# Stick-breaking attention with rounded-and-rest operands for the scores and a balancing rule for the copies

## The chip, the cores and the metric

One core of one Trainium2 chip runs the whole block as one program. The metric is the device time of the program in microseconds; lower is better. The kernel before was run three times: 3305.34, 3305.65 and 3313.6 us, median 3305.65.

## The reference

One layer of a hybrid encoder over 2048 tokens of width 1024, float32: a root-mean-square norm, one input projection, two groups of eight heads (a delta-rule recurrence and stick-breaking attention), one output projection, and a squared-ReLU MLP of width 4096. The change touches only the stick-breaking attention. For a block of 128 queries and all keys up to its end it is

```
z = einsum('bhqd,bhkd->bhqk', q, k) * scale          # head dimension 64
causal = key < query
log_beta = log_sigmoid(z)
log_keep = where(causal, log_beta - z, 0)
log_a = log_beta + reverse_cumsum(log_keep) - log_keep
att = where(causal, exp(log_a), 0)
out = einsum('bhqk,bhkd->bhqd', att, v)
```

So a weight is the sigmoid of a score times the product, over the keys between it and the query, of one minus their sigmoids.

## The kernel before, in words

The program has three stages on one core: stage 1 (norm, input projection, recurrence), stage 2 (the attention, `stage2`), stage 3 (output projection, MLP). Stage 1 writes queries, keys and values to DRAM, two heads to a tile of 128 partitions (64 rows each).

Stage 2 cuts the work into 40 pieces: a pair of heads `hp` (four of them), a block `b` of 512 queries, a block `j` of 512 keys with j from b down to 0. The piece with j equal to b is the diagonal one; 16 pieces are diagonal, 24 are not. A piece is four items, one for each 128 queries, so there are 160 items, counted by `k`. For a diagonal piece item i looks at W = 128(i+1) keys; everywhere else W is 512 ("full"). Of the 160 items, 112 are full.

For each item (lines are those of the kernel before; every instruction of the stage is issued through the helper `call` in `Ordered`, so the profile gives L259 for all of them, and they are told apart by their tiles):

- `scores` (L285): for each of the two heads one float32 matmul of the 64 rows of Q and K into the PSUM tile `z`, two buffers. A float32 matmul is two matmul instructions in the profile.
- `gates` (L293): ScalarE (ACT) computes `keep`, the sigmoid of minus the score, and `ga`, the sigmoid of the score, both from `z` and for both heads at once; on a diagonal item GpSimd (POOL) masks both; VectorE (DVE) runs for each head a reversed running product `E` over `keep`. The scan takes a column of `z` as its second operand.
- `product` (L311): POOL multiplies `ga` by the shifted `E`, one item later.
- Six items later (`lag=6`) the weights are turned: `turn` (L316) lets TensorE (PE) transpose blocks of `ga` into the PSUM tile `tr` (two buffers), and copies it to `th` in SBUF. An item has at most two such parts of 256 queries: the first part's copy runs on ACT, the second's on DVE.
- `values` (L329): PE multiplies `th` with V into the PSUM tile `OT`. `finish` (L338) turns and stores a finished block.

The order is written out by hand: `Ordered` chains all instructions of an engine in program order, so PE, ACT, DVE and POOL each run stage 2 as a fixed queue. One round k of the main loop issues, in this order: transposes and copy of the first part of item k-6; `values` of the second part that was turned in round k-1; the scores of item k; transposes and copy of the second part; the gates and scans of item k; the product of item k-1; and last `values` of the first part. So on PE the order in a round is: transposes of the first part, values of the last round's second part, z(k), transposes of the second part, values of the first part. The main loop's core:

```
first=turn(two[0],A) if two else None
if pend: done=values(*pend) or done
pend=None
z=scores(k) if k<n else None
if len(two)>1: pend=turn(two[1],V_)
if z is not None:
    new=gates(k,z)
    if prod: product(*prod)
    prod=new
...
if first: done=values(*first)
```

K, Q and V come by DMAs on SyncE's queue, issued in `load` by the scores of a piece's first item. Stage 3's first tiles are prepared on DVE, ACT and POOL in between, and its output projection follows when the attention is done.

Of the kernel before, what the change touches and what calls it, by code (L numbers as in the profile page):

```python
# [8 lines left out]
F32 = mybir.dt.float32  # L9
F32R = mybir.dt.float32r  # L10
BF16 = mybir.dt.bfloat16
AF = mybir.ActivationFunctionType
ALU = mybir.AluOpType
# [228 lines left out]
def stage2(tc,consts,kd,qd,vd,sbd,lag=6):  # L242

    nc=tc.nc
    with ExitStack() as ctx:
        sp=ctx.enter_context(tc.tile_pool(name="s2",bufs=1,reuse_waits="tile"))
        pz=ctx.enter_context(tc.tile_pool(name="p2z",bufs=1,reuse_waits="tile",space=PS))
        pp=ctx.enter_context(tc.tile_pool(name="p2",bufs=1,reuse_waits="tile",space=PS))  # L250
        pt=ctx.enter_context(tc.tile_pool(name="p2t",bufs=1,reuse_waits="tile",space=PS,side="right"))
        last={}
        class Ordered:

            def __init__(self,e): self.e=e
            def __getattr__(self,name):
                f=getattr(self.e,name)
                def call(*a,**k):
                    i=f(*a,**k)  # L259
                    if id(self.e) in last:  # L260
                        tc.add_manual_dep(i.ins,last[id(self.e)],mybir.DependencyInfo(mybir.DependencyClass.NoSync,mybir.DependencyReason.DATA),reason="program order")
                    last[id(self.e)]=i.ins.name
                    return i
                return call
        V_,A,P,TE=(Ordered(e) for e in (nc.vector,nc.scalar,nc.gpsimd,nc.tensor))

        keeps=[sp.tile([128,2,513],F32,name=f"keep{i}") for i in range(2)]
        for k in keeps: nc.gpsimd.memset(k[:,:,512:513],1.0)
        class Piece: pass
        pieces=[]  # L270

        for b,hp in [(b,hp) for two in ((0,2),(1,3)) for hp in range(4) for b in two]:
            for j in range(b,-1,-1):
                p=Piece(); p.b,p.hp,p.j,p.n=b,hp,j,f"{b}{hp}{j}"; p.gas=[]; pieces.append(p)
        def load(m):
            p=pieces[m]
            if p.j==p.b:
                p.Q=sp.tile([128,512],F32,tag="Q",name=f"Q{p.b}{p.hp}",bufs=2); p.carry=[None]*4; p.OT=[]
                nc.sync.dma_start(out=p.Q,in_=qd[p.hp][:,512*p.b:512*p.b+512])
            else: p.Q,p.carry,p.OT=pieces[m-1].Q,pieces[m-1].carry,pieces[m-1].OT  # L280
            p.K=sp.tile([128,512],F32,tag="K",name="K"+p.n,bufs=3); p.V=sp.tile([128,4,128],F32,tag="V",name="V"+p.n,bufs=5)
            nc.sync.dma_start(out=p.K,in_=kd[p.hp][:,512*p.j:512*p.j+512])
            nc.sync.dma_start(out=p.V,in_=vd[p.hp][:,4*p.j:4*p.j+4])
        def scores(k):
            p=pieces[k//4]; i=k%4  # L285
            if i==0: load(k//4)
            W=128*(i+1) if p.j==p.b else 512
            z=pz.tile([128,2,512],F32,tag="z",name=f"z{p.n}{i}",bufs=2)
            for h in range(2):
                TE.matmul(z[:,h,0:W],lhsT=p.Q[64*h:64*h+64,128*i:128*i+128],rhs=p.K[64*h:64*h+64,0:W],start=True,stop=True)  # L290
            return z
        def gates(k,z):
            p=pieces[k//4]; i=k%4; diag=p.j==p.b  # L293
            W=128*(i+1) if diag else 512; o=512-W
            s=keeps[k%2]
            A.activation(s[:,:,o:512],z[:,:,0:W],AF.Sigmoid,scale=-0.125)
            ga=sp.tile([128,2,512],F32,tag="ga",name=f"ga{p.n}{i}",bufs=11)
            A.activation(ga[:,:,o:512],z[:,:,0:W],AF.Sigmoid,scale=0.125)
            if diag:

                for t,fill in ((s,1.0),(ga,0.0)):
                    P.affine_select(t[:,:,384:512],t[:,:,384:512],pattern=[[0,2],[-1,128]],base=0,channel_multiplier=1,compare_op=ALU.is_gt,fill=fill)
            E=sp.tile([128,2,513],F32,tag="E",name=f"E{p.n}{i}",bufs=6)

            for h in range(2):
                init=1.0 if diag else p.carry[i][h]
                V_.tensor_tensor_scan(E[:,h,o:513][:,::-1],s[:,h,o:513][:,::-1],z[:,h,0:1].to_broadcast([128,W+1]),init,ALU.mult,ALU.bypass)
            p.carry[i]=[E[:,h,o:o+1] for h in range(2)]
            p.gas.append((ga,o))
            return ga,E,o  # L310
        def product(ga,E,o): P.tensor_tensor(out=ga[:,:,o:512],in0=ga[:,:,o:512],in1=E[:,:,o+1:513],op=ALU.mult)  # L311
        def parts(m):

            p=pieces[m//4]; kt=m%4; i0=kt if p.j==p.b else 0
            return [(p,kt,u,max(i0,2*u)) for u in range(2) if max(i0,2*u)<2*u+2]
        def turn(part,eng):  # L316
            p,kt,u,c0=part

            tr=pt.tile([128,2,256],F32,tag="tr",name=f"tr{p.n}{kt}{u}",bufs=2)
            for h in range(2):  # L320
                for i in range(c0,2*u+2):
                    ga,o=p.gas[i]
                    TE.transpose(tr[:,h,128*(i-2*u):128*(i-2*u)+128],ga[:,h,o+128*kt:o+128*kt+128],consts['ident'])
            th=sp.tile([128,2,256],F32,tag="th",name=f"th{p.n}{kt}{u}",bufs=4)
            q=slice(128*(c0-2*u),256)
            if eng is A: A.copy(th[:,:,q],tr[:,:,q])
            else: V_.tensor_copy(out=th[:,:,q],in_=tr[:,:,q])
            return part,th,q
        def values(part,th,q):  # L329
            p,kt,u,c0=part  # L330
            if p.j==p.b and kt==0 and u==0: p.OT.append(pp.tile([128,512],F32,tag="OT",name=f"OT{p.b}{p.hp}",bufs=2))
            for h in range(2):
                TE.matmul(p.OT[0][64*h:64*h+64,128*c0:256*u+256],lhsT=p.V[:,kt,64*h:64*h+64],rhs=th[:,h,q],start=p.j==p.b and kt==0 and u==0,stop=p.j==0 and kt==3 and u==1,skip_group_check=True)
            if p.j==0 and kt==3 and u==1:
                ots=sp.tile([128,512],F32,tag="ots",name=f"ots{p.b}{p.hp}",bufs=2)
                V_.tensor_copy(out=ots,in_=p.OT[0])
                return p,ots
        def finish(p,ots):  # L338
            o=pt.tile([128,4,128],F32,tag="tr",name=f"o{p.b}{p.hp}",bufs=2)
            for i in range(4): TE.transpose(o[:,i],ots[:,128*i:128*i+128],consts['ident'])  # L340
            osb=sp.tile([128,4,128],F32,tag="osb",name=f"osb{p.b}{p.hp}",bufs=2)
            A.copy(osb,o)
            nc.scalar.dma_start(out=sbd[512*p.b:512*p.b+512,128*p.hp:128*p.hp+128].rearrange("(i p) d -> p i d",i=4),in_=osb)
        n=4*len(pieces); pend=prod=done=out=None
        for k in range(n+lag+2):
            m=k-lag
            two=parts(m) if 0<=m<n else []
            first=turn(two[0],A) if two else None
            if pend: done=values(*pend) or done
            pend=None  # L350
            z=scores(k) if k<n else None
            if len(two)>1: pend=turn(two[1],V_)
            if z is not None:
                new=gates(k,z)
                if prod: product(*prod)
                prod=new
            elif prod: product(*prod); prod=None

            if out: finish(*out)
            out,done=done,None  # L360
            if first: done=values(*first)

# [388 lines left out]
```

## Time and profile before

| What | Value |
|---|---|
| Median of three runs | 3305.65 us |
| Own time of the profiled execution | 3306.65 us |
| Its span, first to last instruction | 3304.9 us |
| Mean granted TensorE clock | 0.976 |
| First scores of stage 2 / last scan of stage 2 starts | 1065.6 us / 1649.0 us |

The profile counts time from the span's start. "Busy" of an engine counts its own instructions, not its waits. A wait is put down to what ended last before the instruction started; that is inferred, and a name can be wrong where the engine named had long been done. Engines: PE is the matmul side of TensorE, PEld its weight loads, DVE VectorE, ACT ScalarE, POOL GpSimd.

### The profile page before, as it was taken

The page shows a single profiled execution, that of the slowest core. Times are in us where ns is not written, and L with a number is a line of the kernel's source. Part 1 is how long each engine was busy: PE and PEld are TensorE (multiplying, and loading weights), DVE is VectorE, ACT ScalarE, POOL GpSimd, SP SyncE. Part 2 cuts the span into 40 slices and gives each one's busy share as a digit, 9 for nine tenths or more (in the row PEclk, how much of TensorE's full clock was granted, in tenths as well). Part 3 has the DMA queues.
Part 4 walks back from the last instruction along what each step waited for, and adds up shares of the span by engine and source line. Part 5 has one row for each costly group of instructions (what it writes and reads, how often), then busy time and mean ns, then how long its engine had stood idle before and what let it go on. Part 6 is the DMA issues. An engine that isn't in the chain of part 4 may idle for free. (4 is left out here: it accounts for less than half of the span.)

```text
span 3304.9 us, 45571 instructions
## 1 busy us (share of the span) xinstructions
PE 3147.4 (95%) x17376; PEld 2373.0 (72%) x17376; DVE 2037.7 (62%) x3157; ACT 1147.4 (35%) x2172; POOL 1293.6 (39%) x1215
## 2 busy tenths in 40 slices
PE   8999999999999798899989999999999999999998
PEld 6677767777777443344467788888888888888887
DVE  4674575476376477888866555555555755555555
ACT  4434443443443366666632221111111411111112
POOL 5444443444443366766646322222221422222213
PEclk9989999999999799999999999999999999999999
DMA  3342242242234212111054121111111511111111
GB/s 100 103 118 75 86 128 77 77 127 86 69 97 119 63 61 68 58 52 58 27 175 161 64 77 51 51 52 52 45 45 45 171 66 51 51 51 46 41 43 64
DMA packets 153643, 251.90 MB, mean 76 GB/s; under 512 B 50768, under 2 KB 58960, under 8 KB 153424
## 3 DMA queue, kind: packets, MB, share of 16 engines
q1 hardware_dynamic: 144976, 244.78, 23.6%
q10 hardware_dynamic: 8448, 4.20, 0.5%
q8 instruction: 137, 2.24, 0.3%
q14 instruction: 82, 0.67, 0.1%
HBM read 202.72 MB, written 46.20 MB: 75 GB/s over the span
## 5 line engine op out<-in xcount | busy, mean ns | idle before, releaser
L158 DVE TENSOR_TENSOR acc<-acc,dn 128x512 f32<-128x512 f32 x512 | 344.5, 685 | 411.3 <-PE dn L32 404.8
L259 POOL TENSOR_TENSOR ga<-ga,E 128x1024 f32<-128x1024 f32 (+3 forms) x160 | 278.4, 1740 | 133.1 <-DVE E L259 76.5
L143 ACT ACTIVATE r<-up 128x512 f32<-128x512 f32 x128 | 75.7, 592 | 615.2 <-PE up L32 615.2
L146 DVE TENSOR_TENSOR m<-r 128x512 f32<-128x512 f32 x128 | 195.2, 1526 | 112.6 <-ACT r L143 112.6
L259 DVE TENSOR_TENSOR_SCAN E<-keep,E,z 128x513 f32<-128x513 f32 x192 | 234.5, 1267 | 45.8 <-ACT ga L259 25.6
L259 PE MATMUL OT<-th,V 128*64 128x256 f32 (+1 forms) x1152 | 183.7, 398 | 39.8 <-DVE th L259 31.2
L259 PEld LDWEIGHTS tr<-ident,ga 128*128 128x128 f32 x1088 | 114.8, 142 | 139.9 <-issue 123.4
L259 ACT ACTIVATE keep<-z 128x1024 f32<-128x1024 f32 (+3 forms) x160 | 144.0, 900 | 155.6 <-PE z L259 75.8
L259 PE MATMUL tr<-ident,ga 128*128 128x128 f32 x1088 | 183.9, 290 | 0.6 <-DVE th L259 0.6
L259 PE MATMUL z<-K,Q 64*128 64x512 f32 (+3 forms) x640 | 163.3, 587 | 19.3 <-DVE E L259 18.6
L147 DVE TENSOR_TENSOR gl<-m,gh 128x512 fp32r<-128x512 f32 x128 | 145.5, 1137 | 10.8
L259 ACT ACTIVATE ga<-z 128x1024 f32<-128x1024 f32 (+3 forms) x160 | 142.9, 893 | 0.0
L259 PEld LDWEIGHTS OT<-th,V 128*64 128x64 f32 x1152 | 57.6, 136 | 109.6 <-DVE th L259 49.9
L405 POOL TENSOR_TENSOR wls<-wfs,whs 128x512 fp32r<-128x512 f32 x64 | 84.7, 1324 | 101.8 <-ACT whs L404 94.7
L555 DVE TENSOR_TENSOR Xs<-Xs,tm 128x240 f32<-128x240 f32 (+27 forms) x248 | 118.5, 478 | 6.3
L554 DVE TENSOR_TENSOR tm<-Am,Xs 128x240 f32<-128x240 f32 (+27 forms) x248 | 103.2, 416 | 23.0 <-DMA Am<-scrA 16.7
L259 DVE TENSOR_TENSOR_SCAN E<-keep,z 128x129 f32<-128x129 f32 (+3 forms) x128 | 98.0, 807 | 26.9 <-ACT ga L259 14.9
L259 DVE COPY th<-tr 128x512 f32<-128x512 f32 x128 | 86.7, 677 | 41.5 <-PE tr L259 41.2
L30 PE MATMUL ips<-hT,whs 128*128 128x512 f32 x256 | 109.0, 426 | 0.0
L32 PE MATMUL ips<-hT,wls 128*128 128x512 f32 x256 | 108.9, 425 | 0.0
L30 PE MATMUL op<-wo,yh 128*128 128x512 f32 x256 | 103.8, 406 | 4.3 <-ACT wo L203 2.3
L31 PE MATMUL op<-wol,yh 128*128 128x512 f32 x256 | 104.1, 407 | 2.4 <-DVE wol L204 2.4
(1261 smaller groups left out, 8651.7 us busy)
## 6 DMA issues: line engine op xcount, KB each, us to landing
wfs<-w_in SPq DMA_DIRECT2D x64, 256.0 KB, 2.8
K<-kd SPq DMA_DIRECT2D x40, 256.0 KB, 2.8
V<-vd SPq DMA_DIRECT2D x40, 256.0 KB, 3.0
x<-x SPq DMA_DIRECT2D x32, 256.0 KB, 3.0
wfr<-w_in SPq DMA_DIRECT2D x32, 256.0 KB, 2.7
wfk<-w_in SPq DMA_DIRECT2D x32, 256.0 KB, 2.7
wfv<-w_in SPq DMA_DIRECT2D x32, 256.0 KB, 2.7
wfsv<-w_in SPq DMA_DIRECT2D x32, 256.0 KB, 2.9
```

What stands on the lines that cost most here:

```text
L30: nc.tensor.matmul(ps,lhsT=lh,rhs=rh,start=first,stop=False)
L31: nc.tensor.matmul(ps,lhsT=lh,rhs=rl,start=False,stop=False)
L32: nc.tensor.matmul(ps,lhsT=ll,rhs=rh,start=False,stop=last)
L143: A.activation(r,ps,AF.Relu)
L146: V.tensor_tensor(out=m,in0=r,in1=r,op=ALU.mult)
L147: V.tensor_tensor(out=gl[:,bl],in0=m,in1=gh[:,bl].bitcast(F32),op=ALU.subtract)
L158: V.tensor_tensor(out=a,in0=a,in1=ps,op=ALU.add)
L259: i=f(*a,**k)
L405: nc.gpsimd.tensor_tensor(out=wl,in0=wf,in1=wh.bitcast(F32),op=ALU.subtract)
L554: V.tensor_tensor(out=tm[:,0:m,i+1:],in0=Am[:,i,i+1:].unsqueeze(1).to_broadcast(sh),in1=X[:,0:m,i:i+1].to_broadcast(sh),op=ALU.mult)
L555: V.tensor_tensor(out=X[:,0:m,i+1:],in0=X[:,0:m,i+1:],in1=tm[:,0:m,i+1:],op=ALU.add)
```

## The change

Four things are done in `stage2`.

1. Scores. Q and K are fetched to `Qf` and `Kf` and split: ACT copies each to a rounded tile (`hi`, type float32r), POOL subtracts it from the original to give the rest (`lo`). A score is then three float32r matmuls accumulated in `z`: hi by hi, hi by lo, lo by hi, with the two heads' matmuls in turn.
2. Fetching. The DMAs of a piece are issued two pieces ahead (in round 2 of a piece), the split one piece ahead (in round 1 of a piece), at the end of the round.
3. Order. `keep` is issued right after the scores, ahead of the second part's transposes and copy; `ga` stays behind them.
4. Copies. Both copies of a round choose their engine by a running count of work: each `keep` adds an item's ACT and DVE work, each split adds 0.58 to ACT, and a copy goes to the engine whose count with the copy added is smaller.

```diff
+        load={"ACT":0.0,"DVE":0.0}
...
-        def load(m):
+        def fetch(m):
             p=pieces[m]
             if p.j==p.b:
-                p.Q=sp.tile([128,512],F32,tag="Q",name=f"Q{p.b}{p.hp}",bufs=2); p.carry=[None]*4; p.OT=[]
-                nc.sync.dma_start(out=p.Q,in_=qd[p.hp][:,512*p.b:512*p.b+512])
-            else: p.Q,p.carry,p.OT=pieces[m-1].Q,pieces[m-1].carry,pieces[m-1].OT
-            p.K=sp.tile([128,512],F32,tag="K",name="K"+p.n,bufs=3); p.V=sp.tile([128,4,128],F32,tag="V",name="V"+p.n,bufs=5)
-            nc.sync.dma_start(out=p.K,in_=kd[p.hp][:,512*p.j:512*p.j+512])
+                p.Qf=sp.tile([128,512],F32,tag="Q",name=f"Q{p.b}{p.hp}",bufs=1); p.carry=[None]*4; p.OT=[]
+                nc.sync.dma_start(out=p.Qf,in_=qd[p.hp][:,512*p.b:512*p.b+512])
+            else: p.Qf,p.carry,p.OT=None,pieces[m-1].carry,pieces[m-1].OT
+            p.Kf=sp.tile([128,512],F32,tag="K",name="K"+p.n,bufs=2); p.V=sp.tile([128,4,128],F32,tag="V",name="V"+p.n,bufs=5)
+            nc.sync.dma_start(out=p.Kf,in_=kd[p.hp][:,512*p.j:512*p.j+512])
             nc.sync.dma_start(out=p.V,in_=vd[p.hp][:,4*p.j:4*p.j+4])
+        def split(m):
+
+            p=pieces[m]
+            two=[("K",p.Kf)]+([("Q",p.Qf)] if p.Qf is not None else [])
+            for t,f in two:
+                hi,lo=(sp.tile([128,512],F32R,tag=t+x,name=t+x+p.n,bufs=2) for x in "hl")
+                A.copy(hi,f); load["ACT"]+=0.58
+                P.tensor_tensor(out=lo,in0=f,in1=hi.bitcast(F32),op=ALU.subtract)
+                setattr(p,t,(hi,lo))
+            if p.Qf is None: p.Q=pieces[m-1].Q
         def scores(k):
             p=pieces[k//4]; i=k%4
-            if i==0: load(k//4)
             W=128*(i+1) if p.j==p.b else 512
             z=pz.tile([128,2,512],F32,tag="z",name=f"z{p.n}{i}",bufs=2)
+            mms=[]
             for h in range(2):
-                TE.matmul(z[:,h,0:W],lhsT=p.Q[64*h:64*h+64,128*i:128*i+128],rhs=p.K[64*h:64*h+64,0:W],start=True,stop=True)
+                r=slice(64*h,64*h+64); q=slice(128*i,128*i+128)
+                mms.append([(p.Q[x][r,q],p.K[y][r,0:W],z[:,h,0:W]) for x,y in ((0,0),(0,1),(1,0))])
+            for c,both in enumerate(zip(*mms)):
+                for l,r,o in both: TE.matmul(o,lhsT=l,rhs=r,start=c==0,stop=c==2,skip_group_check=True)
             return z
+        def keep(k,z):
...
+            A.activation(s[:,:,o:512],z[:,:,0:W],AF.Sigmoid,scale=-0.125)
+            load["ACT"]+=2*(0.1+0.0018*W); load["DVE"]+=2*(0.05+0.0024*W)
         def gates(k,z):
...
-            A.activation(s[:,:,o:512],z[:,:,0:W],AF.Sigmoid,scale=-0.125)
...
-        def turn(part,eng):
+        def turn(part):
...
-            if eng is A: A.copy(th[:,:,q],tr[:,:,q])
-            else: V_.tensor_copy(out=th[:,:,q],in_=tr[:,:,q])
+            w=256*(2-(c0-2*u))
+            if load["ACT"]+0.15+0.0009*w<=load["DVE"]+0.12+0.0011*w: A.copy(th[:,:,q],tr[:,:,q]); load["ACT"]+=0.15+0.0009*w
+            else: V_.tensor_copy(out=th[:,:,q],in_=tr[:,:,q]); load["DVE"]+=0.12+0.0011*w
...
+        fetch(0); split(0); fetch(1)
         n=4*len(pieces); pend=prod=done=out=None
         for k in range(n+lag+2):
             m=k-lag
             two=parts(m) if 0<=m<n else []
-            first=turn(two[0],A) if two else None
+            first=turn(two[0]) if two else None
             if pend: done=values(*pend) or done
             pend=None
             z=scores(k) if k<n else None
-            if len(two)>1: pend=turn(two[1],V_)
+            if z is not None: keep(k,z)
+            if len(two)>1: pend=turn(two[1])
             if z is not None:
                 new=gates(k,z)
...
             if out: finish(*out)
+            if k%4==1 and k//4+1<len(pieces): split(k//4+1)
+            if k%4==2 and k//4+2<len(pieces): fetch(k//4+2)
```

## Rows read from the trace of the kernel before

**Rows 1.** The page: its head and the busy times of PE and DVE.

```profile
span 3304.9 us, 45571 instructions
...
PE 3147.4 (95%) x17376; PEld 2373.0 (72%) x17376; DVE 2037.7 (62%) x3157; ACT 1147.4 (35%) x2172; POOL 1293.6 (39%) x1215
```

**Rows 2.** Busy time by stretch: stage 2, a stretch of stage 3.

```profile
core 0: us, PE busy (x) PEld busy (x) DVE busy (x) ACT busy (x) POOL busy (x), PEclk, DMA share, GB/s
1140.00:1650.00 510.00, 463.81 (x2772) 214.22 (x2772) 410.78 (x452) 334.31 (x476) 322.78 (x275) 0.99 0.18 54
...
2000.00:2400.00 400.00, 400.00 (x1767) 331.34 (x1766) 226.43 (x240) 63.52 (x93) 91.55 (x37) 1.00 0.15 51
```

**Rows 3.** Timeline (start, duration): the round of item 124, item 125 begins.

```profile
1527.68 2.34 DVE L259 TENSOR_TENSOR_SCAN E<-keep,z 128x513 f32<-128x513 f32 x2 [0.82 <-ACT ga L259]
...
1527.82 1.13 PE L259 MATMUL z<-K,Q 64*128 64x512 f32 x4
...
1528.88 0.66 PE L259 MATMUL tr<-ident,ga 128*128 128x128 f32 x4
1529.04 1.03 ACT L259 ACTIVATE keep<-z 128x1024 f32<-128x1024 f32 x1 [0.98 <-POOL ga L259]
...
1529.46 0.65 PE L259 MATMUL OT<-th,V 128*64 128x256 f32 x4
1529.94 0.67 DVE L259 COPY th<-tr 128x512 f32<-128x512 f32 x1
1529.96 1.02 ACT L259 ACTIVATE ga<-z 128x1024 f32<-128x1024 f32 x1
...
1530.05 0.66 PE L259 MATMUL tr<-ident,ga 128*128 128x128 f32 x4
...
1530.66 0.65 PE L259 MATMUL OT<-th,V 128*64 128x256 f32 x4
1530.87 0.59 ACT L259 COPY th<-tr 128x512 f32<-128x512 f32 x1
1531.02 2.46 DVE L259 TENSOR_TENSOR_SCAN E<-keep,E,z 128x513 f32<-128x513 f32 x2 [0.41 <-ACT ga L259]
...
1531.24 1.13 PE L259 MATMUL z<-K,Q 64*128 64x512 f32 x4
...
1533.39 0.66 DVE L259 COPY th<-tr 128x512 f32<-128x512 f32 x1
...
1534.44 2.46 DVE L259 TENSOR_TENSOR_SCAN E<-keep,E,z 128x513 f32<-128x513 f32 x2 [0.39 <-ACT ga L259]
...
1534.69 1.13 PE L259 MATMUL z<-K,Q 64*128 64x512 f32 x4
```

**Rows 4.** Waits, 1140 to 1640 us: who waited for whom, total, times, longest.

```profile
DVE E L259 <- ACT ga L259: 37.4, 60, 1.3
...
PE OT L259 <- DVE th L259: 24.8, 27, 3.2
```

**Rows 5.** Timeline of PE: the score matmuls of item 125, head pairs apart.

```profile
1531.24 0.70 PE L259 MATMUL z<-K,Q 64*128 64x512 f32 x2
...
1531.77 0.60 PE L259 MATMUL z<-K,Q 64*128 64x512 f32 x2
```

**Rows 6.** Groups of instructions by line and shape (busy us, mean ns).

```profile
L405 POOL TENSOR_TENSOR wls<-wfs,whs 128x512 fp32r<-128x512 f32 x64 | 84.7, 1324 | 101.8 <-ACT whs L404 94.7 <-issue 4.0 <-ACT sg L470 2.6
...
L404 ACT CAST whs<-wfs 128x512 fp32r<-128x512 f32 x64 | 39.4, 616 | 70.1 <-issue 20.7 <-PE ips L31 18.8 <-PE ipsv L31 12.4
```

**Rows 7.** Busy time in two stretches of stage 2 (columns of rows 2).

```profile
1127.00:1134.00 7.00, 1.84 (x9) 0.69 (x9) 5.54 (x8) 1.07 (x2) 4.38 (x5) 0.50 0.42 135
...
1345.00:1352.00 7.00, 3.84 (x16) 1.35 (x14) 6.40 (x6) 1.37 (x3) 4.36 (x3) 0.76 0.38 114
```

**Rows 8.** Timeline: where stage 1's last chain ends and stage 2 takes over.

```profile
1113.17 1.91 PE L601 MATMUL Xp<-UV,P 128*64 128x64 f32 x16
...
1115.01 1.12 PE L259 MATMUL tr<-ident,ga 128*128 128x128 f32 x4
```

More of the change, by code (lines that the diff above doesn't have):

```diff
@@ L292, in gates @@
+            return z
+        def keep(k,z):
+            p=pieces[k//4]; i=k%4; diag=p.j==p.b
+            W=128*(i+1) if diag else 512; o=512-W
+            s=keeps[k%2]
+            A.activation(s[:,:,o:512],z[:,:,0:W],AF.Sigmoid,scale=-0.125)
+            load["ACT"]+=2*(0.1+0.0018*W); load["DVE"]+=2*(0.05+0.0024*W)
         def gates(k,z):
```

## The prediction

> **What bounds the kernel now.** I read the head of the page first: TensorE is busy 95% of the span, DVE 62% [rows 1]. A busy PE is not yet the bound, so the stages were read apart. In stage 2, the only one touched, PE is busy 463.8 of 510 us and no other engine over 411 [rows 2]. Then the timeline of one full off-diagonal round, that of item 124 [rows 3]. The reader should see that PE never pauses in it: scores at 1527.82, transposes 1.06 later, values 0.58 after, transposes 0.59, values 0.61, next scores 0.58: 3.42 us a round. But a loop through the other engines is just as long. A scan starts at 1531.02; 2.37 later DVE starts the second part's copy; 0.72 after a copy's start PE starts its values (1529.94 to 1530.66); 0.58 later come the scores; 1.22 after these `keep`, 0.92 later `ga`, 1.06 later the scan. That is 6.87 for two rounds, against 6.84 on PE. Both limits stand together, and a change has to shorten both.
>
> One thing in these rows decides the rest: the scan starts 0.04 after the end of `ga`, not after `keep`, though it reads only `keep`. Over the stage the scans are put down 60 times to `ga` as what ended last [rows 4], and none of the 160 items has a scan that starts ahead of its `ga`'s end. Both read the same PSUM tile `z`, and `ga` stands ahead of the scans in program order, as it does after the change.
>
> Items 0 to 5 run in the shadow of stage 1's last chain, up to 1115 [rows 8]; stage 3 waits for the last attention output. So what a round of stage 2 gains or loses from item 6 on reaches the end.
>
> **Scores.** Removed per full item: two float32 matmuls, each two passes. The first pair of passes (both heads at once) starts at 1531.24, the second at 1531.77 [rows 5]: 0.10 to load weights and 0.43 a pass, so 0.10 + 0.86, and 0.10 more until the transposes: 1.06. Added: three passes in float32r. No float32r matmul on 64 rows is in the trace; the nearest are stage 3's on 128 rows, 400 us for 1767, 0.226 each [rows 2]. If the heads still run together, that is 0.10 + 0.68 + 0.10 = 0.88, a gain of 0.18. The other end is heads in turn, 0.68 more. I take the first, as the float32 pair runs together [rows 5].
>
> Here the Trainium skill speaks against the change. In rows 5 the second pass follows 0.53 after the first, so its weight load lay under the first pass on the same rows of the array. "TensorE: Matmul & The Clock Gate" (Part 3, The mechanism) says that weight loads overlap matmuls in flight "only when row_grp differs". By that rule each later pass of a head would show its load, and the sum below would be +72 instead of +55; the trace disagrees for two passes, and no row shows three.
>
> A round on PE becomes 3.42 - 0.18 = 3.24. For 112 full items that is 20 us; the 32 with 256 or 384 keys give some 0.1 each, 3 us; the 16 with 128 keys I put at nothing, as there weight loads are as long as the passes. Values waited 24.8 us on PE for copies of DVE [rows 4], at the second part. That goes where ACT makes the copy; I take 16, since part of it lies in crowded stretches. Together 39 us less.
>
> **Second copies on ACT.** The rule, worked through with its own constants over the 160 items, gives ACT 101 of the 128 second copies. Such a copy stands between `keep` and `ga`. It holds ACT 0.50 (0.59, less the 0.1 by which ACT's instructions overlap, as 1.03 against 0.92 for `keep`) [rows 3], so `ga` and the scan come 0.50 later. By itself this costs nothing: from scores to scan is then 1.04 + 0.92 + 0.50 + 1.06 = 3.52, and with the scan's 2.46 that is 5.98 for the two `z` buffers, under 6.48. Its own loop (1.04 + 0.92 + copy 0.59 + 0.05 + values 0.58 = 3.18 a round) is just under 3.24.
>
> **First copies on DVE.** The same rule gives DVE 80 of the 160 first copies; all were ACT's. This is the term that decides. On DVE the first copy of round k stands behind the scans of item k-1. On PE its values stand ahead of the next round's transposes, the second part's values and the next scores: PE is in order, so all of these wait. The loop is now: scan to copy 2.37, copy to values 0.72, to transposes 0.59, to values 0.61, to scores 0.58, to `keep` 1.04, to second copy 0.92, to `ga` 0.50, to the scan of item k+1 1.06. That is 8.39 for two rounds, where PE needs 6.48: a price of 1.91 us [rows 3].
>
> It is paid once in two rounds, since a round that follows a held one starts late enough for its own copy. It is full where the scan ahead is 512 wide; behind scans of 128 or 256 it is next to nothing. Of the 80, 49 follow a full scan and no paying round. Five of these lie in the two stretches where stage 3's preparation and its DMAs already hold the stage (PE 1.84 and 3.84 of 7 us [rows 7]); I count nothing for them. 44 x 1.91 = 84 us more. Bounds: 44 x 0.5 if the scan no longer waited for `ga` (a rival below), and 60 x 1.91 = 115.
>
> **Splits.** 40 K and 16 Q tiles: 56 casts on ACT of 0.616 and 56 subtractions on POOL of 1.324 [rows 6], 34 and 74 us of work. ACT is busy 334 and POOL 323 of 510 [rows 2], so they lie beside other work. What can show: the cast is queued behind `ga` and ahead of the next first copy and `keep`. ACT is free 3.38 after a round's scores (1.04 + 0.92 + 0.50 + 0.92); with a first copy and one cast 4.40, with two 4.92, and `keep` is due at 4.28: at most 0.12 in 24 rounds and 0.64 in 15, 12 us. I take 5, as half of these rounds have the first copy on DVE. On POOL the masks of a diagonal item queue behind a subtraction: between 0 and 16 x 1.32 = 21 us; I take 5, because the product ahead of it usually ends early there. The DMAs (same number, same sizes) go out one to two pieces earlier on SP's queue, so K and Q cannot be later than now; nothing. Moving `keep` ahead of the second copy is what lets ACT take it, and costs nothing else.
>
> **Sum.** -39 + 84 + 10 = +55 on the profiled execution's own 3306.65, which is 1.0 over the median: **3361 us**. Stage 2 would end near 1718 instead of 1663.
>
> **Rivals.**
> *The scan is let go by `keep` alone* (the faster side). Then it starts 1.04 + 1.03 + 0.04 = 2.11 after the scores instead of 3.52, a first copy on DVE holds PE only 1.91 - 1.41 = 0.50, and the sum is -39 + 22 + 10 = -7: 3299, astride the bound of 0.3%. For it: `keep` now stands ahead of everything else. Against it: rows 3 and 4, and the order of `ga` and scan is kept.
> *The held values cost nothing*, because something that I read as in order is not; it decides where PE reaches the next scores with the first part's values still waiting. Only the gains stay: 3277. Against it: the stage's order is chained for every engine.
> *Heads in turn*: 0.68 more per full item where PE sets the pace, once in two rounds where the loop does, so 38 to 76: near 3418.
> *Loads that show*: two more loads of 0.10 per full item, with the same discount some 17 us: 3378. Against it: rows 5. It is what the rule of the Trainium skill would do here ("TensorE: Matmul & The Clock Gate", Part 3, The mechanism).
>
> **How the numbers follow.** My forecast 0.62 (its own range 3330 to 3395, from the bounds of price, splits and masks); loads that show 0.08; heads in turn 0.07; scan let go early 0.12; no cost 0.08; anything else 0.03. A measurement of this kernel tells a change of about 0.3%, 10 us, from none. Faster by more: no cost, half of the early scan, and the rest, 0.17. Within: 0.08. Slower: 0.75. The range leaves out the no-cost case and heads in turn: 3285 to 3410.
>
> **What would show it.** In the timeline of a full round: scores to transposes 0.88; the scan 0.04 to 0.1 after `ga`; `ga` 0.50 later behind a second copy on ACT; where DVE has the first copy, values that start 0.7 after that copy's start and a gap of 1.9 on PE ahead of them; scans of item k+1 8.4 behind those of k-1. In the waits of stage 2, "PE OT" or "PEld OT" on "DVE th" near 84 us instead of 25; PE's busy share in stage 2 well under 91%. Wrong would be: scans that start right behind `keep`, rounds of 3.24 with first copies on DVE, or score matmuls whose heads start 0.2 apart.

## The result, and the profile after

The kernel after takes 3415.27 us (median of four executions, 3409.58 to 3416.99), the kernel before 3305.49 in the same comparison: ratio 1.0329, interval 1.0301 to 1.0358. Slower, as forecast, but by 110 us where 55 were forecast, and 5 us beyond the upper end of the range. The execution profiled is that of 3409.58 us.

The head of the page after, busy times and granted TensorE clock in 40 slices of the span (it answers to [rows 1]):

```profile
span 3407.9 us, 46274 instructions
...
PE 3192.9 (94%) x17696; PEld 2433.7 (71%) x17696; DVE 2009.3 (59%) x3136; ACT 1194.9 (35%) x2249; POOL 1363.3 (40%) x1271
...
PEclk9999999999997799888899999999999999999999
```

The span grew by 103.0. Cut at the first scores of item 6 and at the end of the last scan, it goes apart like this:

| Part | Before | After | Difference |
|---|---|---|---|
| up to the scores of item 6 | 1116.06 | 1120.33 | +4.3 |
| from there to the end of the last scan | 534.24 | 633.97 | +99.7 |
| the rest | 1654.6 | 1653.6 | -1.0 |

So nearly all of it lies in stage 2, from item 6 on. Busy time of each engine in that middle part, first of the kernel before, then of the kernel after (columns as in [rows 2]: length, busy time and instructions of PE, PEld, DVE, ACT, POOL, the granted clock, DMA share, GB/s):

```profile
1116.06:1650.30 534.24, 476.80 (x2833) 219.50 (x2832) 423.97 (x467) 344.37 (x488) 331.62 (x284) 0.98 0.19 59
```

```profile
1120.33:1754.30 633.97, 513.97 (x3129) 275.03 (x3128) 405.96 (x446) 386.63 (x558) 393.97 (x335) 0.87 0.17 49
```

Two things are to be seen. PE is busy 81% of it instead of 89%: it waits. And the clock has gone from 0.98 to 0.87. The clock has two levels, 1.2 and 2.4 GHz, so a mean of 0.87 is full speed for 74% of the time and half speed for 26%, or 2 x 0.13 x 634 = 165 us at 1.2 GHz; before it was 2 x 0.02 x 534 = 21 us.

The waits of stage 2 after, 1140 to 1745 us (they answer to [rows 4]: who waited for whom, total, times, longest):

```profile
DVE E L261 <- ACT ga L261: 169.1, 84, 4.4
...
PE OT L261 <- DVE th L261: 89.6, 53, 3.5
```

The timeline of two rounds at full clock, the first with a copy of DVE's ahead of its values (it answers to [rows 3]):

```profile
1501.37 0.50 PE L261 MATMUL z<-Kh,Qh 64*128 64x512 f32 x2
1501.47 0.19 PEld L261 LDWEIGHTS z<-Kl,Qh 64*128 64x128 f32 x2
...
1501.70 0.40 PE L261 MATMUL z<-Kl,Qh 64*128 64x512 f32 x2
1501.70 2.33 DVE L261 TENSOR_TENSOR_SCAN E<-keep,z 128x513 f32<-128x513 f32 x2 [2.03 <-ACT ga L261]
1501.70 0.20 PEld L261 LDWEIGHTS z<-Kh,Ql 64*128 64x128 f32 x2
1501.94 0.40 PE L261 MATMUL z<-Kh,Ql 64*128 64x512 f32 x2
...
1502.26 0.66 PE L261 MATMUL tr<-ident,ga 128*128 128x128 f32 x4
1502.42 1.03 ACT L261 ACTIVATE keep<-z 128x1024 f32<-128x1024 f32 x1 [0.81 <-POOL ga L261]
1503.34 0.58 ACT L261 COPY th<-tr 128x512 f32<-128x512 f32 x1
1503.81 1.04 ACT L261 ACTIVATE ga<-z 128x1024 f32<-128x1024 f32 x1
1503.95 0.66 DVE L261 COPY th<-tr 128x512 f32<-128x512 f32 x1
...
1504.67 0.65 PE L261 MATMUL OT<-th,V 128*64 128x256 f32 x4 [1.75 <-DVE th L261]
1504.88 2.46 DVE L261 TENSOR_TENSOR_SCAN E<-keep,E,z 128x513 f32<-128x513 f32 x2 [0.27 <-ACT ga L261]
...
1506.42 0.50 PE L261 MATMUL z<-Kh,Qh 64*128 64x512 f32 x2
...
1509.65 0.50 PE L261 MATMUL z<-Kh,Qh 64*128 64x512 f32 x2
```

The mechanism is the one forecast. DVE's copy starts at 1503.95, when the scans begun at 1501.70 are done; PE's values follow 0.72 later, after a gap of 1.75. The two rounds start at 1501.37, 1506.42 and 1509.65: 5.05 + 3.23 = 8.28, forecast 8.39. The scan still starts only when `ga` has ended (1503.81 + 1.04 = 1504.85, scan at 1504.88).

Thirty microseconds on, the same pair of rounds (PE and DVE of the timeline):

```profile
1530.18 0.50 PE L261 MATMUL z<-Kh,Qh 64*128 64x512 f32 x2
...
1532.93 0.66 DVE L261 COPY th<-tr 128x512 f32<-128x512 f32 x1
...
1533.65 0.86 PE L261 MATMUL OT<-th,V 128*64 128x256 f32 x4 [1.93 <-DVE th L261]
...
1534.45 1.12 PE L261 MATMUL tr<-ident,ga 128*128 128x128 f32 x4
1535.49 1.12 PE L261 MATMUL OT<-th,V 128*64 128x256 f32 x4
1536.54 0.79 PE L261 MATMUL z<-Kh,Qh 64*128 64x512 f32 x2
...
1540.15 0.50 PE L261 MATMUL z<-Kh,Qh 64*128 64x512 f32 x2
```

The gap on PE is nearly the same, 1.93 against 1.75, but behind it transposes and values take 1.12 where they took 0.65, and the pair takes 6.36 + 3.61 = 9.97. The windows of these 8 us (columns as above):

```profile
1530.00:1534.00 4.00, 2.08 (x18) 1.10 (x14) 3.29 (x4) 2.90 (x4) 2.61 (x2) 0.99 0.25 71
1534.00:1538.00 4.00, 4.00 (x20) 2.01 (x17) 2.21 (x2) 0.61 (x2) 2.81 (x2) 0.58 0.00 0
```

PE worked 2.08 of 4 us while it waited, at a granted clock of 0.99; in the next 4 us it worked without a pause, at 0.58. The wait is paid a second time, in a slower clock when it is over. This is the part that the prediction lacks.

### The profile page after: what moved, and what is told of

It is laid out like the page before. It is cut to its first block, busy times and chain, and to the rows that moved or that the text cites. A ratio compares the mean times of both kernels' runs of the same rounds, so it can differ in the third digit from the quotient of the medians.

```text
span 3407.9 us, 46274 instructions
## 1 busy us (share of the span) xinstructions
PE 3192.9 (94%) x17696; PEld 2433.7 (71%) x17696; DVE 2009.3 (59%) x3136; ACT 1194.9 (35%) x2249; POOL 1363.3 (40%) x1271
## 5 line engine op out<-in xcount | busy, mean ns | idle before, releaser
L261 PE MATMUL OT<-th,V 128*64 128x256 f32 (+1 forms) x1152 | 203.0, 434 | 106.9 <-DVE th L261 96.0
L146 DVE TENSOR_TENSOR m<-r 128x512 f32<-128x512 f32 x128 | 185.0, 1446 | 64.4 <-ACT r L143 64.4
L261 PEld LDWEIGHTS tr<-ident,ga 128*128 128x128 f32 x1088 | 127.8, 154 | 110.2 <-issue 81.8
L261 PE MATMUL tr<-ident,ga 128*128 128x128 f32 x1088 | 204.9, 314 | 1.5 <-ACT th L261 1.5
L261 ACT COPY th<-tr 128x512 f32<-128x512 f32 (+1 forms) x181 | 101.6, 561 | 81.6 <-PE tr L261 80.9
L580 DVE TENSOR_TENSOR Xs<-Xs,tm 128x240 f32<-128x240 f32 (+27 forms) x248 | 110.9, 447 | 6.3
L30 PE MATMUL ips<-hT,whs 128*128 128x512 f32 x256 | 108.4, 423 | 0.5 <-ACT whs L429 0.4
L31 PE MATMUL ips<-hT,whs 128*128 128x512 f32 x256 | 105.3, 411 | 0.0
```

The lines of the kernel that those rows point to most:

```text
L30: nc.tensor.matmul(ps,lhsT=lh,rhs=rh,start=first,stop=False)
L31: nc.tensor.matmul(ps,lhsT=lh,rhs=rl,start=False,stop=False)
L146: V.tensor_tensor(out=m,in0=r,in1=r,op=ALU.mult)
L580: V.tensor_tensor(out=X[:,0:m,i+1:],in0=X[:,0:m,i+1:],in1=tm[:,0:m,i+1:],op=ALU.add)
```

## The experiments

Nine kernels were run, each the kernel after with the edit shown. Ratios are to the kernel before, with their interval. Where an edit hands `turn` an engine, that copy runs there and nothing is weighed. A copy left to the rule goes by the running counts; these count a forced copy on the engine that has it, so a copy left to the rule can change its engine too.

### First copy always on ACT, the second by the rule

```diff
-            first=turn(two[0]) if two else None
+            first=turn(two[0],A) if two else None
```

> The changed kernel, but the first copy of a round always runs on ACT; the second still goes by the rule. Theory (first copies on DVE hold PE, which is in order, for 1.9 us, and in the held rounds the TensorE clock falls): no held rounds are left, rounds take 3.24 us, the granted clock in stage 2 is back above 0.97, and the total is 3265 to 3295 us, below the kernel before. Rival (the three products and the splits cost the time): little changes, 3380 or more. Rival (the clock falls because the scores now give PE less work): the clock stays below 0.92 and the total above 3330.

Measured: 3302.2 us, 1.0001 [0.9992, 1.001]. The whole loss goes when the first copies leave DVE, so the mechanism stands, but more was moved than the first copies: they weigh on ACT's count now, and the rule gives DVE 103 of the 128 second copies instead of 27. The clock of the middle part is back at 0.98, with the same shorter scores, so these alone do not lower it:

```profile
1122.18:1647.51 525.33, 456.39 (x3141) 247.27 (x3140) 406.44 (x442) 381.75 (x564) 392.00 (x335) 0.98 0.19 59
```

The gain expected beyond that did not come, since most second copies are on DVE again, as in the kernel before. The timeline shows what the few on ACT do (rounds begin at 1630.22, 1634.23 and 1637.46):

```profile
1630.22 0.51 PE L261 MATMUL z<-Kh,Qh 64*128 64x512 f32 x2
...
1630.56 2.45 DVE L261 TENSOR_TENSOR_SCAN E<-keep,E,z 128x513 f32<-128x513 f32 x2 [1.47 <-ACT ga L261]
...
1632.93 0.66 DVE L261 COPY th<-tr 128x512 f32<-128x512 f32 x1
...
1633.65 0.65 PE L261 MATMUL OT<-th,V 128*64 128x256 f32 x4 [0.70 <-DVE th L261]
1634.23 0.49 PE L261 MATMUL z<-Kh,Qh 64*128 64x512 f32 x2
...
1637.46 0.50 PE L261 MATMUL z<-Kh,Qh 64*128 64x512 f32 x2
```

A second copy on ACT delays the next scan by 0.5; a second copy on DVE in the round after then stands behind that late scan, and PE waits 0.70 for it. Here the rule makes them alternate, and two rounds take 4.01 + 3.23 = 7.24, more than the 6.84 of before. I had costed each engine's copies alone, not their alternation.

### First copy on ACT, second on DVE, as before

```diff
-            first=turn(two[0]) if two else None
+            first=turn(two[0],A) if two else None
...
-            if len(two)>1: pend=turn(two[1])
+            if len(two)>1: pend=turn(two[1],V_)
```

> The changed kernel with the old assignment of the copies: first on ACT, second on DVE. So the three products, the splits and the early fetches alone. Theory: the loop scan, second copy on DVE, values, scores, keep, ga, scan is 6.69 for two rounds, 3.35 a round against 3.44 before; total 3285 to 3315, clock as before (0.97 or more in stage 2). Rival (products and splits cost the time): 3380 or more.

Measured: 3295.27 us, 0.9977 [0.9965, 0.9989]. The three products, the splits, the earlier fetch and the earlier `keep` together gain 8 to 10 us. They are not what makes the kernel slow.

### The rule alone, with float32 scores

The kernel after with the scores of before, and no splits (their weight in the count is kept):

```diff
-                for l,r,o in both: TE.matmul(o,lhsT=l,rhs=r,start=c==0,stop=c==2,skip_group_check=True)
+                TE.matmul(z[:,h,0:W],lhsT=p.Q[64*h:64*h+64,128*i:128*i+128],rhs=p.K[64*h:64*h+64,0:W],start=True,stop=True)
```

> The kernel before with the rule for the copies, keep issued early and the early fetches, but float32 scores and no splits (the rule's counts are kept as in the changed kernel, so the copies go to the same engines). Theory: held rounds as in the changed kernel, two rounds 8.6 us against 6.84; 44 holds of 1.7 us less 16 is +60 at full clock, and 20 to 60 more from the clock: 3380 to 3430. Rival (products and splits cost the time): 3295 to 3315. Rival (the clock falls because the scores give PE less work): held rounds, but the clock at 0.97, 3355 to 3370.

Measured: 3382.45 us, 1.0249 [1.023, 1.0268]. The rule, with the early fetch and the early `keep`, makes 79 of the 110 us. But that leaves a sum that does not close: -10 for the products and +79 for the rule make +69, and together they make +110. (The early fetch and the early `keep` are in both runs, so what they do is counted twice in this sum; the run with all copies on ACT and float32 scores, further down, settles it.) The missing 40 us need a cause that grows when the scores get shorter. The clock is one: in the middle part it is 0.94 here and 0.87 in the kernel after.

```profile
1116.25:1729.03 612.78, 498.60 (x2829) 228.41 (x2828) 405.29 (x447) 360.50 (x507) 331.71 (x284) 0.94 0.16 51
```

### A scan that doesn't read the scores' tile

The scan's second operand, which it does not use, is taken from `keep` instead of `z`:

```diff
-                V_.tensor_tensor_scan(E[:,h,o:513][:,::-1],s[:,h,o:513][:,::-1],z[:,h,0:1].to_broadcast([128,W+1]),init,ALU.mult,ALU.bypass)
+                V_.tensor_tensor_scan(E[:,h,o:513][:,::-1],s[:,h,o:513][:,::-1],s[:,h,512:513].to_broadcast([128,W+1]),init,ALU.mult,ALU.bypass)
```

> The changed kernel, but the scan takes its unused second operand from keep's own tile in SBUF and no longer from z. Theory (the scan waits for ga because both read z): scans start 0.04 to 0.1 after keep ends, a first copy on DVE holds PE 0.5 us instead of 1.9, the clock stays above 0.95, total 3280 to 3320. Rival (the scan waits for ga for another reason): scans still start after ga, total near 3410. Open: scans with two operands from SBUF may get in POOL's way; then scans or products grow longer than 1.27 and 2.00 us.

Measured: 3467.72 us, 1.0504 [1.0486, 1.0521]: far slower, and no test of the time; the clock fell too (0.86 from 1140 to 1640 us). It shows one thing all the same. In half of the 160 items the scans now start ahead of the end of `ga`, by up to 1.49 us, and in the kernel after in none, so the shared tile was what held them. But two other things got longer (groups by shape, 1140 to 1640 us: busy, mean ns of one):

```profile
L261 DVE TENSOR_TENSOR_SCAN E<-keep,E 128x513 f32<-128x513 f32 x136 | 282.2, 2121 | 17.3 <-ACT keep L261 17.2
L261 POOL TENSOR_TENSOR ga<-ga,E 128x1024 f32<-128x1024 f32 x79 | 189.8, 2404 | 74.8 <-DVE E L261 61.1 <-ACT keep L261 7.3 <-PE tr L261 5.2
```

The same groups of the kernel after, 1140 to 1745 us:

```profile
L261 DVE TENSOR_TENSOR_SCAN E<-keep,E,z 128x513 f32<-128x513 f32 x188 | 230.4, 1268 | 119.8 <-ACT ga L261 112.0 <-issue 5.7 <-POOL Kl L261 2.1
L261 POOL TENSOR_TENSOR ga<-ga,E 128x1024 f32<-128x1024 f32 x109 | 218.1, 2002 | 127.6 <-DVE E L261 114.8 <-ACT th L261 4.5 <-ACT Kh L261 4.3
```

A scan went from 1.268 to 2.121 us and a product from 2.002 to 2.404 once both operands of the scan lay in SBUF. The column of `z` is no oversight of the kernel before: it keeps the scan off something that it would share with POOL. The Trainium skill says so ("SBUF — State Buffer", Who interferes with whom): a DVE instruction with two SBUF inputs contends with a GpSimd instruction that reads SBUF. The trace agrees, and the single scans tell more than these means: the 38 full scans that meet no work of POOL's take 1.26 us, and the 86 that start inside one product and meet no other end 1.08 to 1.09 us after it, however much of it was left. So a scan waits for the whole rest of the product, as one would expect of the exclusive lock of which the Trainium skill speaks in the same section. One of them (product, then scan):

```profile
1665.45 1.99 POOL L261 TENSOR_TENSOR ga<-ga,E 128x1024 f32<-128x1024 f32 x1
...
1665.53 3.00 DVE L261 TENSOR_TENSOR_SCAN E<-keep,E 128x513 f32<-128x513 f32 x1
```

### All copies on ACT

```diff
-            first=turn(two[0]) if two else None
+            first=turn(two[0],A) if two else None
...
-            if len(two)>1: pend=turn(two[1])
+            if len(two)>1: pend=turn(two[1],A)
```

> The changed kernel with every copy of turned weights on ACT. Theory: neither the hold of 1.9 us nor the alternation seen with first copies fixed (4.01 and 3.23 us: a second copy on ACT delays a scan, and the next second copy, on DVE, waits behind it) is left; PE sets the pace with 3.24 to 3.28 us a round, total 3255 to 3285, clock 0.97 or more. Rival (ACT becomes the bound with 2.84 us a round plus the casts): rounds of 3.4 or more, total above 3295.

Measured: 3275.31 us, 0.9908 [0.9889, 0.9928]. As expected, and faster than both kernels. It stands to the kernel of the second experiment in the second copies alone, which are thus worth 20 us on ACT. Its middle part takes 500.7 us at a clock of 0.98:

```profile
1124.29:1625.00 500.71, 455.71 (x3147) 247.63 (x3147) 349.14 (x344) 428.57 (x662) 392.14 (x335) 0.98 0.21 62
1458.68:1618.97 160.29, 151.80 (x1061) 82.16 (x1059) 112.20 (x106) 142.48 (x217) 122.28 (x100) 1.00 0.15 45
```

Now ACT has 80% more copies than in the kernel before, and PE's values wait for them only 6.0 us in 26 waits, the longest 0.4 (1140 to 1640 us): in a queue in which the work falls due in the order in which it stands, no balance was needed.

### All copies on ACT, with float32 scores

The edits of the third experiment and of the last one together; the scores are then those of before again.

> The kernel before with early keep and early fetches, float32 scores, no splits, and every copy on ACT. Theory: PE sets the pace with 3.42 us a round and the waits of values on DVE are gone: total 3280 to 3297; the difference to the run with three products and all copies on ACT is 112 x 0.18 = 20 us less what the casts cost. Rival (the gain of the other run came from the copies alone): the two are equal.

Measured: 3281.83 us, 0.9935 [0.992, 0.9951], as expected. The three products with their splits are worth 6.5 us over it. And it gives the price of the rule against all copies on ACT with either kind of scores: 612.78 - 515.64 = 97 us of the middle part with float32 scores, and 633.97 - 500.71 = 133 with three products. All four kernels have the early fetch and the early `keep`, so nothing is counted twice here, and some 36 us are still left that neither the rule nor the products make alone.

```profile
1114.32:1629.96 515.64, 475.71 (x2839) 220.12 (x2839) 349.65 (x344) 405.11 (x611) 331.27 (x284) 0.99 0.20 61
```

### Work for TensorE while it waits

One float32 matmul of 512 columns, into an output block that is written over later, is put in each held round ahead of the values that wait (49 in all). The blocks `OT` share one tile for this.

```diff
+            TE.matmul(OTs[:,runs[0]%2],lhsT=consts['ident'],rhs=part[0].V.rearrange("p a b -> p (a b)"),start=True,stop=True)
...
+            if first and first[3] and runs[0]: fill(k,first[0])
             if first: done=values(*first)
```

> The changed kernel with one extra float32 matmul of 512 columns (about 1 us) on PE ahead of the values of a first part that DVE copies, in 49 rounds where PE waits 1.7 to 1.9 us there; it writes to a PSUM bank that nobody reads. The output blocks share one tile of two banks instead of two buffers. Theory (PE's idle time in held rounds lets the clock fall, and that is what the forecast left out): holds as before, 8.3 us for two rounds, but the granted clock in stage 2 above 0.95, total 3345 to 3380. Rival (the clock costs nothing, since PE waits anyway): the total stays at 3405 or more, whatever the clock does; extra work on PE may even make it longer.

Measured: 3387.02 us, 1.0251 [1.023, 1.0271]. Seven over the range, but on the side that tells: the kernel does all the work of the kernel after and more, and takes 28 us less. Its held pairs at full clock are unchanged (8.29). I put the seven down to fillers that wait at the end of an output block, such as this one, and tried that next.

```profile
1513.42 2.07 PE L261 MATMUL OTs<-V,ident 128*128 128x512 f32 x2 [2.43 <-DVE ots L261]
```

### The same, but not where an output block ends

```diff
-            if first and first[3] and runs[0]: fill(k,first[0])
+            if first and first[3] and runs[0] and not done and not out: fill(k,first[0])
```

> The kernel after with the extra float32 matmul on TensorE in held rounds, as in the run before with fillers, but left out of the rounds in which an output block ends, where it waited for a copy of that block. If the lower clock is what lengthens the held rounds beyond 8.3 us for two, then more work on TensorE must make the kernel shorter again: holds still 8.2 to 8.4 us for two rounds, mean granted clock of stage 2 (1140 us to its end) at 0.94 or more, 3350 to 3390 us in all. If the lower clock costs nothing and the extra lies in the held copies themselves, nothing is won over the kernel after: 3405 us or more. If the waits for the output block's copy were not the price of the first fillers, the same as with these, 3387.

Measured: 3390.01 us, 1.0257 [1.0241, 1.0273]: at the upper edge of the clock's range and the same as with the first fillers. Whether their waits were the price this does not tell, because the waits stayed. The output blocks share one tile in both kernels with fillers, and now it is the values of the next block that wait for the copy of the finished one (waits 1140 to 1745 us; 15.9 us in 9 waits with the first fillers, none in the kernel after):

```profile
PE OTs L261 <- DVE ots L261: 16.2, 9, 2.4
```

So the 28 and 25 us that the two kernels with fillers win are won in spite of these waits. Leaving some fillers out did shorten the middle part, by 8.7 us in the executions profiled, while the rest of the program was 5.6 us longer in this one. The clock of the middle part is 0.95, not 1.00 (first the kernel with all fillers, then this one):

```profile
1122.95:1741.59 618.64, 519.38 (x3233) 267.48 (x3234) 406.01 (x447) 385.74 (x558) 393.45 (x335) 0.94 0.17 51
```

```profile
1122.71:1732.64 609.93, 510.78 (x3221) 266.52 (x3222) 405.87 (x447) 385.23 (x558) 392.62 (x335) 0.95 0.17 51
```

But the run gave what was wanted, a long stretch in which the same holds run at full clock: items 108 to 159, from scores to scores. First this kernel, then the kernel after:

```profile
1534.45:1726.62 192.17, 164.77 (x1088) 86.03 (x1086) 129.79 (x138) 128.19 (x183) 122.75 (x99) 1.00 0.12 38
```

```profile
1536.54:1748.27 211.73, 177.74 (x1061) 94.89 (x1060) 128.95 (x137) 128.81 (x182) 122.59 (x99) 0.86 0.12 34
```

The same copies on the same engines, 27 more matmul instructions, and 19.6 us less: with the clock at 1.00 PE is busy 13 us less for more work. At 0.86 the kernel after spends 2 x 0.14 x 211.7 = 59 us of this stretch at 1.2 GHz, so a microsecond at the lower clock cost 19.6 / 59 = 0.33. The Trainium skill reckons half of such time as lost ("TensorE: Matmul & The Clock Gate", HAM oscillation — how this bites in real kernels); an estimate by that is 30 us of the 59. The measured 19.6 decides. It is rather low, as four of the waits for the output block, 7.8 us in all, lie in this stretch; for the rest, PE need not be on the path all the time, which no run shows by itself.

All copies on ACT take 160.29 for these items, also at 1.00, so the rule at full clock costs 31.9 us here, with what the fillers cost. Of this, 26.8 us lie in 14 held rounds of 5.06 to 5.51 us: they are 1.7 to 2.2 us longer than the same rounds with all copies on ACT, 1.91 in the mean, which is the price forecast.

### The casts on DVE

All copies on ACT, and the casts of K and Q on DVE:

```diff
-                A.copy(hi,f); load["ACT"]+=0.58
+                V_.tensor_copy(out=hi,in_=f); load["ACT"]+=0.58
```

> All copies of the turned weights on ACT, and the casts of K and Q on DVE instead of ACT. Theory: the rounds of 3.83 us in the version with all copies on ACT are those in which a cast stands on ACT ahead of the next first copy; with the casts on DVE, which then has only the scans (two of 1.23 us in a round of 3.23), they become 3.23 and the whole is 3255 to 3272 us. Rival: a cast on DVE stands behind a scan and so makes POOL's subtraction, and with it the diagonal items' masks, later, or DVE's cast and POOL's work slow each other as the scans with two SBUF operands did: no gain, 3275 us or more.

Measured: 3284.6 us, 0.9938 [0.9924, 0.9951]: the time is the rival's. The rounds with two casts do become 3.23 (items 110 and 111 begin at 1471.83 and 1475.06), but the scan of the diagonal item behind them comes later (timeline, POOL and DVE):

```profile
1475.18 1.29 POOL L261 TENSOR_TENSOR Kl<-K,Kh 128x512 fp32r<-128x512 f32 x1 [1.64 <-DVE Kh L261]
...
1476.42 1.28 POOL L261 TENSOR_TENSOR Ql<-Q,Qh 128x512 fp32r<-128x512 f32 x1
1477.66 3.96 POOL L261 TENSOR_TENSOR ga<-ga,E 128x1024 f32<-128x1024 f32 x2
...
1481.57 0.41 POOL L261 TENSOR_SCALAR_AFFINE_SELECT keep<-keep 128x256 f32<-128x256 f32 x1
...
1482.01 0.74 DVE L261 TENSOR_TENSOR_SCAN E<-keep,z 128x129 f32<-128x129 f32 x2 [0.92 <-POOL keep L261]
```

Casts that wait for DVE's scans make POOL's subtractions late, the products queue behind these, the mask of the diagonal item behind the products, and its scan waits for the mask: it starts 3.7 us after its scores, with the casts on ACT 2.7. Yet no round is longer for it here, and items 108 to 119 together win 1.2 us. The loss lies elsewhere: items 98, 122 and 146, with 384 keys, take 0.5 to 0.6 us longer each than with the casts on ACT, and items 6 to 15 and 62 to 75 take 1.8 and 1.0 us longer in all. The middle part is 2.9 us longer than with the casts on ACT, its start 3.2 later. That masks made late are the cause is thus shown for a scan, and not for the loss.

## Why the prediction was right or wrong

**Right: the bound, the mechanism and its place.** PE's order is the loop; DVE's first copies hold it. The gap is 1.75 to 1.93 in the rounds shown, the pair of rounds 8.28 against 8.39, PE's wait for DVE's copies 89.6 us in stage 2 against 84 forecast. Scans begin when `ga` ends, so the early-scan rival (3299) falls, and the no-cost rival with it.

**Right: the scores.** From scores to transposes it is 0.89 (1501.37 to 1502.26; forecast 0.88). The passes start 0.33 and 0.24 apart for both heads together, so heads in turn falls, and so do loads that show: the weight loads of the second and third pass (1501.47 and 1501.70) lie under the passes ahead of them, on the same rows, against the rule that the prediction weighed (the Trainium skill, "TensorE: Matmul & The Clock Gate", Part 3, The mechanism).

**Right as a sum, by terms that shift, and so partly by luck.** "-39" and "+10" made -29; all copies on ACT has both and gives -30. In it the second copies on ACT are worth 20 (forecast 16), and the products with all that goes with them 10 (forecast 23 less 10). Of the splits' 10, some 3 lay where I put them: six rounds with two casts take 3.80 instead of 3.23 with all copies on ACT. The rest may lie elsewhere: the kernels with splits begin item 6 at 1120 to 1127 us, the ones without at 1114 to 1116. What delays that start was not followed up.

**Wrong: "44 x 1.91 = 84".** This is the step that failed. It prices a held round at full clock, and the text says nothing of the clock. Count and price themselves come out about right: in the middle part of the trace after, 40 values wait longer than 1.5 us for a copy of DVE's, and a held round at full clock costs 1.91 (items 108 to 159, above). What is missing is what comes on top. In the middle part the rule costs 633.97 - 500.71 = 133 us. The kernel after is at 1.2 GHz for 165 us of it, all copies on ACT for 2 x 0.02 x 500.7 = 20; at 0.33 the difference of 145 is 48 us. That leaves 85 for the holds themselves, near the 84 forecast. The 0.33 is measured for items 108 to 159; carried to the whole part it is an estimate, and other pairs of runs give others. The kernel with the second fillers has a middle part 24 us shorter than the kernel after and 104 us less at 1.2 GHz, 0.23; the rule costs 36 us more with three products than with float32 scores, at 82 us more of 1.2 GHz, 0.44. So the clock makes 33 to 64 of the 133, and the holds 100 to 69. With float32 scores the same working gives 2 x (0.06 x 612.8 - 0.01 x 515.6) x 0.33 = 21 of the 97 us, and 76 for the holds. By this estimate the part that did not add up in the third experiment is mostly clock, which is low for 165 us instead of 74. My reading is that shorter scores leave PE less to do beside the same wait; it takes both, as the clock is 0.98 with the same scores and no held rounds.

The rows to see it were there: [rows 7] has PE busy 1.84 of 7 us at a clock of 0.50, and 3.84 of 7 at 0.76. I read them as stretches that others hold, and not as what a waiting PE does to its own clock. The forecast with 48 for this term would have been +103.

**Open.** Some waits can change sides when the clock falls, so 48 and 85 are not exact. No run has separate output blocks and fillers, which would show what the shared tile costs. The fillers left the clock of items 6 to 107 below 1, so no run has every hold at full clock.

## What to carry to other kernels

A wait on TensorE that comes back again and again can be paid more than once: price it with the granted clock of a stretch where PE already waits like that, and not at full speed. Balance work between two in-order engines by when each one's queue reaches it and who stands behind it, not by the sum of work: here the rule kept ACT and DVE nearly even (387 and 406 us busy in the middle part) and the copies on DVE came late, while all copies on ACT, then the busier one (429 against 349), gave the fastest kernel. When two parts of a change don't add up, look for the resource that both of them touch.

## What was not expected of the hardware

- With waits of 1.75 to 1.93 us on PE in one of two rounds the granted clock fell again and again: 0.87 in a stage where PE was busy 81%. With one more matmul in the waits it was 0.94 and 0.95.
- A scan with both operands in SBUF ran 2.121 us instead of 1.268 beside POOL's products, and these 2.404 instead of 2.002. A scan that starts inside a product ends 1.08 us after it; alone it takes 1.26.
- Three float32r passes of 512 columns on 64 rows, for two heads, take 0.97 us with all their weight loads, 0.16 less than the two passes of float32 (1.13 [rows 3]).
